# Gate and up units in a seven-product feed-forward: two of four weight sums made by one accumulating transfer, and two small moves beside it

## The chip, the cores and the metric

The kernel runs on one core of a Trainium2 chip. Its time is the device time of one execution in microseconds; lower is better. The engines are called here PE (TensorE), ACT (ScalarE), DVE (VectorE), POOL (GpSimd) and SP (SyncE, which only issues transfers).

## The reference

Two layers of a hybrid decoder trunk on x of 512 rows by 1024 features, in float32. Each layer is

```
x = x + 1/2 * SwiGLU_1(RMSNorm(x))
h = RMSNorm(x);  [conv_a | conv_g | q | k | v] = h @ W_in
x = x + concat(conv_out, diff_out) @ W_out
x = x + 1/2 * SwiGLU_2(RMSNorm(x))

def swiglu(h, w_gate, w_up, w_down):
    return (jax.nn.silu(h @ w_gate) * (h @ w_up)) @ w_down
```

The hidden width of the feed-forwards is 2816, that is 22 tiles of 128. conv_out is a causal depthwise convolution of width 31 behind a gate, diff_out a differential attention with a shared relative-position bias. All matrix products are carried to nearly float32 precision.

## The kernel before

**Products in three parts.** PE multiplies numbers of a rounded 32-bit type (fp32r). So each operand is split into a rounded part (hi, a copy on ACT) and the remainder (lo, a subtraction on DVE), and each product is made as hi by hi, lo by hi and hi by lo. The helper `mm3` (L138, L141, L142) does it for whole tiles of 512 columns, `Unit.product` (L377) for halves of 256 columns.

**A feed-forward** (`ffn`, four in the kernel) has three parts. The first five hidden tiles are plain: a product with the gate and one with the up weights, silu and product on DVE and ACT, hi and lo of the result (`hh`, `hl`: `Gated.plain`, L600 and L601), and eight down products of five tiles each into `ps_d`, added to x at L706. Beside that, `Halves` makes the sums of the two halves of the normed input (L309 to L318), and `settle` its hi and lo parts `acth` and `actl` (L323, L324). Then come two groups, of 8 and of 9 hidden tiles, each followed by four `Down` units. A `GateUp` unit makes one hidden tile's gate and up product with seven products of 256 columns instead of eight, as in Winograd's form of a two by two block product; a `Down` unit does so for two output tiles.

**The weights of a unit.** `GateUp.load` (L455) brings the up weights u and the gate weights g by two transfers of SP, 512 KB each (L457, L458), and POOL makes four sums of them (`sums`, L354 to L357): D = g1 + u1, u1 + u2, u1 + u2 + g1, and that plus g2, where 1 and 2 are the halves of the contracted dimension. `hi` (L363, ACT) and `lo` (L367, DVE) then split the four sets: A (u1 + u2 and u2), B (g), C (the last two sums) and D. Buffers come from rings: `wraw` has five of 128x1024, `whi` and `wlo` four, `wraw2`, `whi2` and `wlo2` (512 wide) two.

**Order.** `Unit.body` (L390) runs one unit and, in between its products, the preparation of the next: load, then hi and lo of A (after the first products, copied at L395), B, D and C. In between go the last product of the unit before (`rest`) and its elementwise work (`finish`, `extras`). Copies of partial sums out of PSUM go to `keep` (L395, L406, L426). A scheduler reorders the instructions of the program by its own model of time; only the first matmul of each product group is held in the order of the program. Each engine runs its stream in order.

**Other places that the steps touch.** `Gated.add` (L607) makes, for the first of a pair of hidden tiles, the difference of the two halves of the activation (L618); the held copy of the activation comes from PSUM one step earlier. `Down.plain` (L540) adds the products of hidden tiles that are in no pair; `middle` (L556) issues the ones for the first bank before the unit's last two product groups. `close` (L565) adds the partial sums (L570) and adds the result to x (L561). The bias table of the attention (`make_bias`) is built beside the first feed-forward; one of its steps is a transfer `d<-d` (L747) on POOL's queue.

Of the kernel before, what the change touches and what calls it, by code (L numbers as in the profile page):

```python
# [14 lines left out]
AF = mybir.ActivationFunctionType  # L15
ALU = mybir.AluOpType
AX = mybir.AxisListType

P = 128
# [27 lines left out]
PIN = False  # L47
# [21 lines left out]
def trunk(ctx: ExitStack, tc: tile.TileContext, xt, par, lamv, relb, onehot,  # L69
          gu1, dn1, wag, wqkv, wout, gu2, dn2, out):  # L70
    nc = tc.nc
    V, S, G, T = nc.vector, nc.scalar, nc.gpsimd, nc.tensor
# [9 lines left out]
    def f32(ap):  # L82
        return ap.bitcast(F32)
# [9 lines left out]
    def ring(tag, n=1024):  # L93
        dt = F32 if "raw" in tag else F32R
        return wp.tile([P, n], dt, tag=tag, name=tag, bufs=RING[tag])
# [70 lines left out]
    for k0, k1 in ((0, 1), (1, 4), (4, KT)):  # L166
        h = slice(k0 * P, k1 * P)
# [48 lines left out]
    class Prep:  # L216


        def __init__(self, l, gain):
            self.l, self.gain = l, gain  # L220
            self.hi, self.lo = acth, actl
            self.s = tmp.tile([P, SEQ], F32, tag="ssum", name="ssum", bufs=1)
# [110 lines left out]
    def pinned(ins, pin=PIN):  # L333
        if pin:
            tc.keep_in_program_order(ins)
        return ins
# [4 lines left out]
    def by_two(t):  # L341
        return t.rearrange("p (n c) -> p n c", n=2)

    class Unit:
# [14 lines left out]
        def hi(self, k, pin=PIN):  # L359
            tag, n = self.WIDE[k]  # L360
            hi, lo = ring("whi" + tag, n), ring("wlo" + tag, n)
            self.parts[k] = hi, lo
            pinned(S.activation(hi[:, : self.cols[k]], self.raw[k][:, : self.cols[k]], AF.Copy), pin)  # L363

        def lo(self, k, pin=PIN):
            (hi, lo), c = self.parts[k], self.cols[k]
            pinned(V.tensor_tensor(out=lo[:, :c], in0=self.raw[k][:, :c], in1=f32(hi[:, :c]), op=ALU.subtract), pin)  # L367
# [22 lines left out]
        def body(self, nxt, prev, prev2):  # L390
            if nxt:
                nxt.load()
            self.begin()
            self.go(self.c, "u2u1", "t1", first=True)
            pinned(S.activation(self.keep[:, 3], self.c, AF.Copy))  # L395
            if nxt:
                nxt.hi("A")
                nxt.lo("A")
            self.go(self.d, "u2", "t4", first=True)
            self.early()  # L400
            if nxt and self.early_free:
                nxt.hi("B")
            if prev:
                prev.rest()
            self.go(self.a, "g1", "b11")
            pinned(S.activation(self.keep[:, :2], by_two(self.banks[0]), AF.Copy))  # L406
            if prev:
                prev.finish(0)
            if nxt and self.early_free:
                nxt.lo("B")  # L410
            if prev:
                prev.finish(1)
            if nxt:
                nxt.hi("D")
                nxt.lo("D")
            if prev:
                prev.finish(2)
            self.go(self.b, "g2", "b21")
            self.middle()
            if nxt:  # L420
                nxt.hi("C")
            if prev2:
                prev2.extras()
            self.go(self.c, "all", "b22")
            self.go(self.a, "g1u2u1", "t2")
            pinned(S.activation(self.keep[:, 2], self.a, AF.Copy))  # L426
            self.close()
            if nxt:
                nxt.lo("C")
                if not self.early_free:  # L430
                    nxt.hi("B")
                    nxt.lo("B")

        early_free = True

        def early(self):
            pass

        def middle(self):
            pass  # L440
# [6 lines left out]

    class GateUp(Unit):
        steps = KT // 2

        def __init__(self, fp, turn, halves, g, u, n, gated):
            super().__init__(fp, turn)
            self.halves, self.src, self.n, self.gated = halves, (g, u), n, gated

        def load(self):  # L455
            u, g = ring("wraw"), ring("wraw")
            nc.sync.dma_start(u, self.src[1])  # L457
            nc.sync.dma_start(g, self.src[0])  # L458
            d, more = ring("wraw2", 512), ring("wraw")
            h = slice(0, 512), slice(512, 1024)  # L460
            self.sums(u[:, h[0]], u[:, h[1]], g[:, h[0]], g[:, h[1]], d, more[:, h[0]], more[:, h[1]])
            self.raw = {"A": u, "B": g, "C": more, "D": d}
            self.cols = {k: n for k, (_, n) in self.WIDE.items()}

        AT = {"u2u1": ("A", 0), "u2": ("A", 4), "g1": ("B", 0), "g2": ("B", 4), "g1u2u1": ("C", 0), "all": ("C", 4),
              "g1u1": ("D", 0)}
# [8 lines left out]
        def close(self):  # L475
            g, two = self.keep[:, 0::2], by_two(self.banks[1])
            pinned(V.tensor_tensor(two, two, g, op=ALU.add))
            pinned(S.activation(g, two, AF.Silu))
# [14 lines left out]
    class Down(Unit):  # L493
# [60 lines left out]
                self.spare()  # L554

        def middle(self):  # L556
            if self.early_free:
                self.plain(self.banks[1], 0)

        def into(self, m, ps, scale):  # L560
# [4 lines left out]
        def close(self):  # L565
            A, B = 2 * self.q, 2 * self.q + 1
            two, keep = by_two(self.banks[1]), self.keep
            if not self.early_free:
                self.plain(self.banks[1], 0)
            pinned(V.tensor_tensor(two, two, keep[:, 0::2], op=ALU.add))  # L570
            self.into(A, two, 0.5)
            self.after(A)
            if not self.early_free:
                self.spare()
            two = by_two(self.ps)
            pinned(V.tensor_tensor(two, two, keep[:, 1::2], op=ALU.subtract))
            self.into(B, two, 0.5)
# [7 lines left out]
    class Gated:  # L585
# [21 lines left out]
        def add(self, n, us, step):  # L607
            a, b = slice(0, HS), slice(HS, SEQ)
            first = self.paired(n) and n % 2 == 0
            if step == 0:  # L610
                if first:
                    self.held[n] = self.fp.tile([P, SEQ], F32, tag=("hh8", "hl8")[n // 2 % 2], name="hold")
                    pinned(S.activation(self.held[n], us, AF.Copy))
                else:
                    self.part_hi(n, us)
            if step == 1:
                if first:
                    pinned(V.tensor_tensor(us[:, b], self.held[n][:, a], self.held[n][:, b], op=ALU.subtract))  # L618
                    self.part_hi(n, us)
                else:  # L620
                    self.part_lo(us)
            if step == 2 and first:
                self.part_lo(us)
# [481 lines left out]
    for l in range(DEPTH):  # L1105
        nxt = {}
# [89 lines left out]
```

## Time and profile before

| | |
|---|---|
| median of the runs | 1791.06 us (1789.68, 1791.06, 1792.72) |
| the profiled execution | 1787.99 us |
| its span | 1786.2 us, 1.8 us less than its time |
| granted clock of PE | 0.999 |
| PE busy | 1771.4 us, 99% |
| DVE, ACT, POOL busy | 1416.0, 960.1 and 950.4 us (79, 54 and 53%) |
| read from HBM | 173.79 MB |

Busy time counts the execution of an engine's instructions. A group's row gives busy time, count and mean, and then the time that the engine sat idle just before, with what ended it. A row of the timeline gives start, duration, engine and line. A row of the waits gives the total, the number of times and the longest, all in us.

### The profile page before, as it was taken

Reading aid. Unit: us, or ns where it says so; the run is one execution under the profiler, and the core shown is the slowest. Engines: PE = TensorE matmul, PEld = TensorE weight load, DVE = VectorE, ACT = ScalarE, POOL = GpSimd, SP = SyncE. Lnnn points to the kernel's source line nnn. Section 1 sums busy time; section 2 is a strip of 40 time slices with the busy share of each in tenths; the row PEclk is TensorE's granted clock in tenths of the full one; section 3 lists DMA queues with packets and bytes.
Section 4 is the critical chain, followed back from the end, with each engine's and each line's share of the span. In section 5 each row is a group of like instructions: output and inputs, shape, how many; then the busy total and the mean of one; then the engine's idle time right before and its main releaser. Section 6 shows DMA issues by size and latency. Waiting matters only on the chain.

```text
span 1786.2 us, 29641 instructions
## 1 busy us (share of the span) xinstructions
PE 1771.4 (99%) x11437; PEld 1608.5 (90%) x11437; DVE 1416.0 (79%) x1949; ACT 960.1 (54%) x1555; POOL 950.4 (53%) x665
## 2 busy tenths in 40 slices
PE   9999999999999999999999999999999999999998
PEld 7899999888788899999888999998877888999997
DVE  6988797768857978798668978976788588887974
ACT  5455465545844456465534654655558354554652
POOL 2275475279952166475304745742798432654750
PEclk9999999999999999999999999999999999999999
DMA  7333334423122233333332333344230232333332
GB/s 224 95 113 97 105 107 113 128 91 95 48 71 83 83 95 118 85 113 120 107 97 71 107 107 99 103 119 130 71 116 26 72 106 73 106 97 105 107 108 70
DMA packets 74222, 177.83 MB, mean 100 GB/s; under 512 B 8951, under 2 KB 30726, under 8 KB 74080
## 3 DMA queue, kind: packets, MB, share of 16 engines
q1 hardware_dynamic: 72480, 174.10, 31.9%
q8 instruction: 89, 1.46, 0.3%
q0 software_dynamic: 1312, 1.67, 0.3%
q14 instruction: 53, 0.43, 0.1%
q10 hardware_dynamic: 288, 0.16, 0.0%
HBM read 173.79 MB, written 3.42 MB: 99 GB/s over the span
## 4 chain that ended last, share of the span: by engine, by line
PE 96%; DVE 2%; ACT 1%; issue 0%; DMA 0%; SPq 0%; DVEq 0%; ACTq 0%
PE ps_pair L377 53%; PE ps_d L377 6%; PE ps_pair L141 5%; PE ps_pair L142 5%; PE ps_pair L138 5%; PE ps_d L138 2%; PE ps_d L142 2%; PE ps_d L141 2%; PE ps_sc L966 2%; PE ps_pair L842 2%; PE ps_pair L843 2%; PE ps_pair L844 2%; PE ps_out L138 1%; PE ps_out L142 1%; PE ps_out L141 1%; PE ps_v L872 1%
## 5 line engine op out<-in xcount | busy, mean ns | idle before, releaser
L367 DVE TENSOR_TENSOR wlo<-wraw,whi 128x1024 fp32r<-128x1024 f32 (+2 forms) x400 | 534.6, 1342 | 122.0 <-ACT whi L363 120.2
L363 ACT ACTIVATE whi<-wraw 128x1024 fp32r<-128x1024 f32 (+2 forms) x400 | 361.5, 909 | 354.6 <-PE ps_pair L377 188.3
L354 POOL TENSOR_TENSOR wraw<-wraw 128x512 f32<-128x512 f32 (+1 forms) x100 | 145.1, 1451 | 540.9 <-DMA wraw<-in_gu 279.4
L377 PE MATMUL ps_pair<-acth,wlo 128*128 128x256 f32 x1088 | 307.9, 283 | 0.0
L377 PE MATMUL ps_pair<-actl,whi 128*128 128x256 f32 x1088 | 307.9, 283 | 0.0
L377 PE MATMUL ps_pair<-acth,whi 128*128 128x256 f32 x1088 | 307.9, 283 | 0.0
L377 PE MATMUL ps_pair<-th,whi 128*128 128x256 f32 x816 | 231.7, 284 | 0.0
L377 PE MATMUL ps_pair<-th,wlo 128*128 128x256 f32 x816 | 230.9, 283 | 0.0
L377 PE MATMUL ps_pair<-tl,whi 128*128 128x256 f32 x816 | 230.9, 283 | 0.0
L377 PEld LDWEIGHTS ps_pair<-acth,whi 128*128 128x128 f32 x1088 | 208.9, 192 | 0.2
L377 PEld LDWEIGHTS ps_pair<-actl,whi 128*128 128x128 f32 x1088 | 208.9, 192 | 0.2
L377 PEld LDWEIGHTS ps_pair<-acth,wlo 128*128 128x128 f32 x1088 | 208.9, 192 | 0.0
L101 ACT ACTIVATE whi<-wraw 128x1024 fp32r<-128x1024 f32 (+3 forms) x124 | 122.6, 999 | 144.4 <-PE ps_pair L141 87.3
L141 PE MATMUL ps_pair<-actl,whi 128*128 128x512 f32 x448 | 174.7, 391 | 0.7 <-DVE actl L227 0.5
L142 PE MATMUL ps_pair<-acth,wlo 128*128 128x512 f32 x448 | 174.1, 390 | 0.0
L138 PE MATMUL ps_pair<-acth,whi 128*128 128x512 f32 x448 | 173.2, 392 | 0.4 <-ACT whi L101 0.4
L356 POOL TENSOR_TENSOR wraw<-wraw 128x512 f32<-128x512 f32 (+1 forms) x100 | 154.0, 1540 | 7.8
L377 PEld LDWEIGHTS ps_pair<-th,whi 128*128 128x128 f32 x816 | 156.6, 192 | 0.9
L357 POOL TENSOR_TENSOR wraw<-wraw 128x512 f32<-128x512 f32 (+1 forms) x100 | 153.2, 1532 | 7.8
L377 PEld LDWEIGHTS ps_pair<-tl,whi 128*128 128x128 f32 x816 | 156.6, 192 | 0.0
L377 PEld LDWEIGHTS ps_pair<-th,wlo 128*128 128x128 f32 x816 | 156.6, 192 | 0.0
L355 POOL TENSOR_TENSOR wraw<-wraw 128x512 f32<-128x512 f32 (+1 forms) x100 | 148.1, 1481 | 7.8
(203 smaller groups left out, 4307.5 us busy)
## 6 DMA issues: line engine op xcount, KB each, us to landing
wraw<-in_gu SPq DMA_DIRECT2D x172, 512.0 KB, 3.6
wraw<-in_wqkv SPq DMA_DIRECT2D x24, 512.0 KB, 3.6
wraw<-in_wag SPq DMA_DIRECT2D x16, 512.0 KB, 3.6
wraw<-in_wout SPq DMA_DIRECT2D x16, 512.0 KB, 3.6
wraw<-in_dn SPq DMA_DIRECT2D x60, 128.0 KB, 3.0
wraw<-in_dn SPq DMA_DIRECT2D x20, 384.0 KB, 3.3
wraw<-in_dn SPq DMA_DIRECT2D x28, 256.0 KB, 2.9
wraw<-in_dn SPq DMA_DIRECT2D x20, 320.0 KB, 3.1
```

Source lines behind the costliest of these rows:

```text
L101: S.activation(hi, raw, AF.Copy)
L138: first = T.matmul(ps, wh, xh, start=start, stop=False)
L141: T.matmul(ps, wh, xl, start=False, stop=False)
L142: T.matmul(ps, wl, xh, start=False, stop=stop)
L354: G.tensor_tensor(d, g1, u1, op=ALU.add)
L355: G.tensor_tensor(u1, u1, u2, op=ALU.add)
L356: G.tensor_tensor(m0, u1, g1, op=ALU.add)
L357: G.tensor_tensor(m1, m0, g2, op=ALU.add)
L363: pinned(S.activation(hi[:, : self.cols[k]], self.raw[k][:, : self.cols[k]], AF.Copy), pin)
L367: pinned(V.tensor_tensor(out=lo[:, :c], in0=self.raw[k][:, :c], in1=f32(hi[:, :c]), op=ALU.subtract), pin)
L377: mm = T.matmul(ps, l, r, start=first and i == n == 0, stop=False, skip_group_check=True)
L842: T.matmul(ps[n], xh[:, t], wh, start=k == 0, stop=False)
```

## The change

`GateUp.load` issues four transfers of SP: gate's first half and up's second half into the two halves of a buffer `two`, the whole gate weights into `g`, and up's second half once more into a 512-wide buffer. One transfer on POOL's queue then adds up's first half to both halves of `two` while it is written, which gives D and the first half of A. POOL makes the two remaining sums. A now lies in two buffers, and its hi and lo are made in two instructions of 512 columns each. For units that prepare a `GateUp` unit, the hi and lo of A come later in the body, behind `finish(1)` and ahead of D. The difference at L618 (L646 after) takes its second operand from PSUM instead of from the held copy. In the last `Down` unit of each feed-forward the plain products of the first bank are issued in `close` and not in `middle`.

```diff
--- before.py
+++ after.py
@@ -393,7 +393,7 @@
             self.begin()
             self.go(self.c, "u2u1", "t1", first=True)
             pinned(S.activation(self.keep[:, 3], self.c, AF.Copy))
-            if nxt:
+            if nxt and nxt.soon:
                 nxt.hi("A")
                 nxt.lo("A")
             self.go(self.d, "u2", "t4", first=True)
@@ -411,6 +411,9 @@
             if prev:
                 prev.finish(1)
             if nxt:
+                if not nxt.soon:
+                    nxt.hi("A")
+                    nxt.lo("A")
                 nxt.hi("D")
                 nxt.lo("D")
             if prev:
@@ -432,6 +435,7 @@
                     nxt.lo("B")
 
         early_free = True
+        soon = True
 
         def early(self):
             pass
@@ -447,20 +451,44 @@
 
     class GateUp(Unit):
         steps = KT // 2
+        soon = False
 
         def __init__(self, fp, turn, halves, g, u, n, gated):
             super().__init__(fp, turn)
             self.halves, self.src, self.n, self.gated = halves, (g, u), n, gated
 
         def load(self):
-            u, g = ring("wraw"), ring("wraw")
-            nc.sync.dma_start(u, self.src[1])
-            nc.sync.dma_start(g, self.src[0])
-            d, more = ring("wraw2", 512), ring("wraw")
             h = slice(0, 512), slice(512, 1024)
-            self.sums(u[:, h[0]], u[:, h[1]], g[:, h[0]], g[:, h[1]], d, more[:, h[0]], more[:, h[1]])
-            self.raw = {"A": u, "B": g, "C": more, "D": d}
-            self.cols = {k: n for k, (_, n) in self.WIDE.items()}
+            gate, up = self.src
+            two, g, u2 = ring("wraw"), ring("wraw"), ring("wraw2", 512)
+            nc.sync.dma_start(two[:, h[0]], gate[:, h[0]])
+            nc.sync.dma_start(two[:, h[1]], up[:, h[1]])
+            nc.sync.dma_start(g, gate)
+            nc.sync.dma_start(u2, up[:, h[1]])
+            nc.gpsimd.dma_start(
+                by_two(two), up[:, h[0]].unsqueeze(1).broadcast_to([P, 2, 512]), accum_op=ALU.add
+            )
+            more = ring("wraw")
+            G.tensor_tensor(more[:, h[0]], two[:, h[1]], g[:, h[0]], op=ALU.add)
+            G.tensor_tensor(more[:, h[1]], more[:, h[0]], g[:, h[1]], op=ALU.add)
+            self.raw = {"A": (two[:, h[1]], u2), "B": (g,), "C": (more,), "D": (two[:, h[0]],)}
+
+        def pieces(self, k):
+            at = 0
+            for raw in self.raw[k]:
+                n = raw.shape[1]
+                yield raw, *(p[:, at : at + n] for p in self.parts[k])
+                at += n
+
+        def hi(self, k, pin=PIN):
+            tag, n = self.WIDE[k]
+            self.parts[k] = ring("whi" + tag, n), ring("wlo" + tag, n)
+            for raw, hi, _ in self.pieces(k):
+                pinned(S.activation(hi, raw, AF.Copy), pin)
+
+        def lo(self, k, pin=PIN):
+            for raw, hi, lo in self.pieces(k):
+                pinned(V.tensor_tensor(out=lo, in0=raw, in1=f32(hi), op=ALU.subtract), pin)
 
         AT = {"u2u1": ("A", 0), "u2": ("A", 4), "g1": ("B", 0), "g2": ("B", 4), "g1u2u1": ("C", 0), "all": ("C", 4),
               "g1u1": ("D", 0)}
@@ -554,7 +582,7 @@
                 self.spare()
 
         def middle(self):
-            if self.early_free:
+            if self.early_free and not self.last:
                 self.plain(self.banks[1], 0)
 
         def into(self, m, ps, scale):
@@ -565,7 +593,7 @@
         def close(self):
             A, B = 2 * self.q, 2 * self.q + 1
             two, keep = by_two(self.banks[1]), self.keep
-            if not self.early_free:
+            if not self.early_free or self.last:
                 self.plain(self.banks[1], 0)
             pinned(V.tensor_tensor(two, two, keep[:, 0::2], op=ALU.add))
             self.into(A, two, 0.5)
@@ -615,7 +643,7 @@
                     self.part_hi(n, us)
             if step == 1:
                 if first:
-                    pinned(V.tensor_tensor(us[:, b], self.held[n][:, a], self.held[n][:, b], op=ALU.subtract))
+                    pinned(V.tensor_tensor(us[:, b], self.held[n][:, a], us[:, b], op=ALU.subtract))
                     self.part_hi(n, us)
                 else:
                     self.part_lo(us)
```

## Prediction

> **What bounds the kernel now.** I read the page's busy times and chain first, then the list of what TensorE (PE) waits for, then the longest pieces of the chain, then the grouped rows of the engines that the change touches, and last the timeline at the places where the order changes.
>
> ```profile
> PE 1771.4 (99%) x11437; PEld 1608.5 (90%) x11437; DVE 1416.0 (79%) x1949; ACT 960.1 (54%) x1555; POOL 950.4 (53%) x665
> PE 96%; DVE 2%; ACT 1%; issue 0%; DMA 0%; SPq 0%; DVEq 0%; ACTq 0%
> PE ps_pair L377 <- ACT keep L426: 3.2, 3, 1.4
> PE ps_v L872 <- ACT qz L888: 1.8, 1, 1.8
> 90.65 87.87 PE ps_pair L377 x720
> ```
>
> PE is busy 99% of the span and is 96% of the chain. The fifth line is a stretch of the gate/up units: 720 half-width products in 87.87 us, 0.122 us each without a gap, so a unit of 7 x 12 = 84 products takes 10.25 us, whatever VectorE (DVE), ScalarE (ACT), GpSimd (POOL) and the transfers do underneath. The change removes and adds no product. It can gain only what PE waits for, of which the largest entry is the 3.2 us before L377, and it can lose without limit if a weight or an activation comes late.
>
> **The moved plain products: the gain.** The last Down unit of each feed-forward sends its plain products (5 x 3 at 128x512) ahead of the last pair's reconstruction; after the change they stand between the copy L426 (L429 after) and the last products that need it.
>
> ```profile
> 316.99 3.43 PE ps_d L377 x15
> 350.90 0.28 PE L377 MATMUL ps_pair<-hs,wlo 128*128 128x256 f32 x1
> 352.54 0.50 PE L377 MATMUL ps_pair<-hs,whi 128*128 128x256 f32 x2 [1.35 <-ACT keep L426]
> 1780.90 0.50 PE L377 MATMUL ps_pair<-hs,whi 128*128 128x256 f32 x2 [0.47 <-ACT keep L426]
> 1780.88 0.70 DVE L570 TENSOR_TENSOR ps_pair<-ps_pair,keep 128x512 f32<-128x512 f32 x1 [3.94 <-ACT keep L426]
> 356.70 2.69 POOL L239 TENSOR_TENSOR ssum<-ssum,sq 128x512 f32<-128x512 f32 x2 [2.21 <-ACT sq L235]
> 360.19 0.60 PE L196 MATMUL ps_rows<-ident,ssum 128*128 128x128 f32 x4
> ```
>
> The first line sizes the moved block, 3.43 us of PE. At 350.90 PE waits 1.35 us for the copy, and the same 1.35 us comes again in layer 1 (3.2 = 1.35 + 1.35 + 0.47). A block of 3.43 us covers it, so both waits go: -2.7 us. What is late next there is the row of squares: PE's transposes of it ran at 360.19 and POOL's last sum (L239) ends at 359.39; that chain also moves up, so I count the gain as whole and its loss (0 of 2.7) as the lower bound. At the end of the kernel the final subtraction L570 starts when the copy is there (1780.88); after the change it is PE that ends last, at about 1780.45 without its wait of 0.47, so 0.4 us at most and 0.3 taken. At the fourth place, the passage from layer 0 to layer 1, no wait stands in the list, so nothing. Sum -3.0 us, at least 0, at most -3.4.
>
> **PSUM instead of SBUF for one difference (L618).**
>
> ```profile
> L618 DVE TENSOR_TENSOR ps_pair<-hold 128x256 f32<-128x256 f32 x16 | 24.4, 1522 | 0.0
> L484 DVE TENSOR_TENSOR ps_pair<-ps_pair,keep 128x256 f32<-128x256 f32 x68 | 28.6, 421 | 0.1
> ```
>
> The same shape with a PSUM operand takes 421 instead of 1522 ns: 16 x 1.1 = 17.6 us of DVE. DVE is not on the chain there, since PE runs these stretches without a gap: nothing.
>
> **The four sums and the accumulating transfer.**
>
> ```profile
> L354 POOL TENSOR_TENSOR wraw<-wraw 128x512 f32<-128x512 f32 x68 | 116.8, 1717 | 370.6 <-DMA wraw<-in_gu 279.4 <-issue 35.7 <-DVE wlo L367 21.6
> L357 POOL TENSOR_TENSOR wraw<-wraw 128x512 f32<-128x512 f32 x68 | 125.5, 1845 | 5.3
> L367 DVE TENSOR_TENSOR wlo<-wraw,whi 128x1024 fp32r<-128x1024 f32 x268 | 396.1, 1480 | 103.3 <-ACT whi L363 101.9
> L367 DVE TENSOR_TENSOR wlo<-wraw,whi 128x512 fp32r<-128x512 f32 x116 | 125.6, 1083 | 18.7 <-ACT whi L363 18.3
> L363 ACT ACTIVATE whi<-wraw 128x1024 fp32r<-128x1024 f32 x268 | 283.9, 1060 | 281.4 <-PE ps_pair L377 138.6 <-PE ps_d L377 56.8 <-POOL wraw L356 26.5
> L363 ACT ACTIVATE whi<-wraw 128x512 fp32r<-128x512 f32 x116 | 72.9, 628 | 67.5 <-PE ps_pair L377 44.1 <-POOL wraw L354 16.9 <-DVE wlo L367 2.7
> q1 hardware_dynamic: 72480, 174.10, 31.9%
> wraw<-in_gu SPq DMA_DIRECT2D x172, 512.0 KB, 3.6
> d<-brow POOLq DMA_DIRECT2D x1, 8.0 KB, 1.7
> d<-d POOLq DMA_DIRECT2D x1, 1280.0 KB, 19.7
> ```
>
> In each of 68 units POOL loses two of four sums and keeps about 3.6 us (two of these rows). A's hi and lo in two halves cost ACT 2 x 0.63 for 1.06 (+0.2 us a unit) and DVE 2 x 1.08 for 1.48 (+0.7, less what two fewer POOL sums give back). Both have room: nothing. SP issues four loads of 1.25 MB for two of 1 MB, and with the accumulating 0.5 MB a unit moves 1.75 times as much; the hardware queue takes 31.9% of the 16 engines now, so bandwidth is there. What is new is that POOL issues a transfer and waits for it before its two sums, and that it issues the next only after them. With L the time from issue to landing, POOL's loop lasts L + 3.6 and must not exceed 10.25: L up to 6.65 costs no lag at all. No accumulating transfer is in the trace. From below: a plain hardware transfer of the size takes 3.6. From above: the one large transfer on POOL's queue took 19.7 us for 1280 KB, 7.9 for 512 KB, and with 1.7 for a small one 9.6. I take 5.5: 1.7 fixed, and two reads of 512 KB at the 1.9 us (3.6 less 1.7) of one. This lies under 6.65, so in the steady stretch nothing, and the range keeps the upper end.
>
> The row that this leans on is the 3.6 us of a plain transfer. The Trainium skill, page "Collectives: The Full Stack", section "The bandwidth ceiling: the fold count and why AG ≠ RS ≠ AR", says that an adding transfer reads two sources through one ring and so moves at half the rate (62.28 against 32.35 GB/s there). By it alone the data part would double, the L that I take; no run here shows it yet.
>
> There is also lead before a lag hurts. The row order of one unit:
>
> ```profile
> 114.88 1.45 DVE L367 TENSOR_TENSOR wlo<-wraw,whi 128x512 fp32r<-128x512 f32 x1
> 113.12 0.58 ACT L478 ACTIVATE keep<-ps_pair 128x512 f32<-128x512 f32 x1
> ```
>
> A unit's first pair is now loaded when this lo of D frees its buffer (116.3), lands 3.6 later (119.9), and A's hi is due right after the L478 slot (113.7) two bodies on, at 134.2: 14.3 us, some 16.5 with the 2.3 us that I estimate ACT can slip. A transfer of L plus lags of L - 6.65 over 5 (group of eight) or 6 (group of nine) loops must fit: L up to 8.3 and 8.1.
>
> **The start of a feed-forward: the cost.** The instruction streams say where the first unit's D is converted. In the first feed-forward its hi on ACT, and its lo on DVE, now stand ahead of the plain weights' hi (L101), of the plain units' hh (L600) and of the hi of the normed activations; before they stood behind hh. Both engines run in order, so all of that now waits for the first accumulating transfer.
>
> ```profile
> 44.76 1.15 POOL L747 DMA_DIRECT2D d<-d  x1 [1.75 <-DMA d<-brow]
> 64.78 1.85 POOL L354 TENSOR_TENSOR wraw<-wraw 128x512 f32<-128x512 f32 x1 [18.87 <-DMA wraw<-in_gu]
> 50.33 0.33 SPq L457 DMA_DIRECT2D wraw<-in_gu  x1
> DMA to landing us min/median/max: 3.4/3.6/12.4
> 58.79 0.61 ACT L600 ACTIVATE hh<-gs 128x512 fp32r<-128x512 f32 x1
> 66.67 0.63 ACT L363 ACTIVATE whi<-wraw 128x512 fp32r<-128x512 f32 x1 [3.71 <-POOL wraw L354]
> 64.65 0.62 PE L138 MATMUL ps_d<-hh,whi 128*128 128x512 f32 x2
> 65.78 0.39 PE L141 MATMUL ps_d<-hl,whi 128*128 128x512 f32 x1
> L102 DVE TENSOR_TENSOR wlo<-wraw,whi 128x1024 fp32r<-128x1024 f32 x67 | 86.1, 1292 | 37.1 <-ACT whi L101 37.1
> L633 DVE TENSOR_TENSOR hl<-ps_pair,hh 128x512 fp32r<-128x512 f32 x68 | 46.3, 680 | 5.3 <-ACT hh L628 5.3
> ```
>
> The unit's load at 50.33 is the slow one (12.4 us, landed 62.7), beside the bias table's d<-d, which is on POOL's queue from 44.76 to 64.46. The accumulating transfer can only be asked for at 62.7 or a little later and stands behind d<-d on the same queue. It lands at X: at the earliest 64.5 + 1.7 = 66.2, at the latest 64.5 + 5.5 = 70; I take 68.5. From X follow D's hi (0.6), its lo (1.1), the weights' lo (L102, 1.3) and hl (L601, 0.7 as L633): hl is there at X + 3.7, and PE, which read it at 65.78, stands X - 62.1 = 6.4 us (4.1 to 7.9). The hi side, X + 2.2 against 64.65, gives 6.0. These are waits of PE that nothing hides: +6.4 us.
> ```profile
> 1501.52 0.63 ACT L600 ACTIVATE hh<-gs 128x512 fp32r<-128x512 f32 x1 [7.12 <-DVE gs L689]
> 1502.73 1.07 PE L138 MATMUL ps_d<-hh,whi 128*128 128x512 f32 x4
> ```
>
> At the other three starts no bias table is in the way and the load lands in 3.6 us. The tightest tile there is the last hh, ready at 1502.15 and read among the four products from 1502.73, so with about 0.8 us of slack: 0 to 1 us each, I take +0.5 in all.
>
> The two mixers' products come in another order in the stream as well (a scheduler places them); the largest of PE's waits there is the 1.8 us of the row quoted first, so I put this at 0, from -1.5 to +2.
>
> **Sum.** -3.0 + 6.4 + 0.5 = +3.9 us on the profiled execution (span 1786.2, 1.8 around it, 1787.99). It lies 3.1 under the median of the runs, 1791.06; I add the difference to the median: **1795.0 us**. About 0.2% (3.6 us) is what a measurement of this kernel can tell from no change.
>
> **Rivals.**
> 1. No stall at the start (0.2): the transfer gets ahead of the tail of d<-d, or lands by 62.5 or so because the pair's loads are smaller. Then the gain is alone: 1791.06 - 3.0 = 1788.0, with a friendly mixer order 1786.5. Against it: the 12.4 us and d<-d's end at 64.46.
> 2. The accumulating transfer is slow (0.17): L beyond 8.1 makes POOL's loop the bound in all four feed-forwards. At L = 8.5 a group of eight is late by 51.0 - 49.8 = 1.2, of nine by 59.5 - 56.4 = 3.1, four of each 17 us: on top of the forecast, 1812. At 9.6 it is 7.8 + 10.8, times four 74 us: 1869. For it: the d<-d row. Against: that transfer's outermost dimension is short, the new one runs over 128 partitions.
> 3. The start stalls but less, X at 66.2 (0.2): 4.1 instead of 6.4, with mixers at -1: 1791.
>
> Forecast as above, 0.43: 1793 to 1798. Faster by over 0.2% needs both no stall and a good order of the mixers, or the gain at the passages larger than its waits: 0.18. Within 0.2%: 0.27 (most of rival 3 and the rest of rival 1, the low part of the forecast). Slower: 0.55 (the rest of the forecast, rival 2). The range, 1787.0 to 1812, leaves out the good end of rival 1 and most of rival 2.
>
> **What would show it.** Right: in the list of PE's waits the entry for the copy L429 shrinks to under 0.6 us, and a new one of 4 to 8 us stands before ps_d L138 or L141 near 65 us, put down to hh or hl; the gate/up stretch stays at 87.87 us; the DMA issues show the accumulating transfer at 5 to 6 us. Wrong: no gap near 65 (rival 1), or PE gaps before L377 that recur from unit to unit, released by whi L487, with the landing above 8 us (rival 2). A shift in the mixers at equal waits would mean that the order of their products counted for more than I gave it.

## The result, and the profile after

The changed kernel takes 1808.95 us, median of five runs (1808.36 to 1811.45), against 1790.19 us (1789.17 to 1792.72) for the kernel before: a ratio of 1.0109, 95% interval 1.0097 to 1.0120. It is 18.8 us slower; 1795.0 was forecast, with a range from 1787.0 to 1812.

The page of the changed kernel, busy times and chain:

```profile
PE 1778.5 (98%) x11437; PEld 1610.4 (89%) x11437; DVE 1329.0 (74%) x2017; ACT 963.6 (53%) x1623; POOL 768.6 (43%) x597
PE 87%; DVE 6%; DMA 5%; issue 1%; ACT 1%; SPq 0%; DVEq 0%; POOLq 0%; ACTq 0%
```

POOL lost 182 us of work and DVE 87 us, and the kernel became slower: neither was what it waited for. The chain now spends 11% on DVE and transfers, where before PE had nearly all of it. That is not 11% lost, since PE worked beside most of it. What PE waits for (total, times, longest), changed kernel:

```profile
PE ps_d L138 <- ACT hh L628: 8.7, 3, 7.1
PE ps_d L138 <- DVE x L734: 4.8, 3, 2.7
PE ps_v L900 <- ACT qz L916: 1.8, 1, 1.8
```

The 3.2 us on the copy L429 are gone. Two new entries stand before `ps_d`, the plain down products at the start of a feed-forward. The long pieces of the chain show that nothing happened inside the groups:

```profile
51.50 12.64 DMA wraw<-in_gu
64.83 5.69 DMA wraw<-in_gu
88.88 5.63 DMA wraw<-in_gu
105.26 87.87 PE ps_pair L377 x720
```

720 products still take 87.87 us; they begin at 105.26 instead of 90.65. The three lines ahead of it are what stands in the way: the first unit's load, its accumulating transfer, and the second unit's accumulating transfer.

Both kernels run the same number of products on PE, outside the mixers almost in the same order. So the start times can be subtracted product by product. By how much each stretch is longer than in the kernel before (minus: shorter), in us, profiled executions of the changed kernel and of the experiments:

```
                     changed  small_  accum_  sums_   sums_   move_   bias_   late_d
                              edits   only    first1  first2  some    wide
before 49.5 us          0.80    1.80    1.79    0.06    0.08    0.45    0.04    0.87
start, 1st ff          13.82    0.00   12.27    2.29    0.00    0.00    7.81    0.00
its end                -1.62   -1.61    0.00   -1.62   -1.62   -1.61   -1.61   -1.61
mixer, layer 0          0.40    1.05    0.67    1.01    2.82    1.90    2.49    1.47
start, 2nd ff           2.02    0.00    1.73    0.21    0.00    0.00    2.34    0.00
start, 3rd ff           1.57    0.00    2.31    0.81    0.00    0.00    1.87    0.00
its end                -1.61   -1.61    0.00   -1.61   -1.61    0.00   -1.61   -1.61
mixer, layer 1          2.19    3.85   -0.05    2.17    2.19   -0.09    2.20    3.87
start, 4th ff           3.28    0.00    2.27    0.06    0.00    0.00    2.57    0.00
end                    -0.73   -0.73    0.00   -0.73   -0.73   -0.73   -0.73   -0.73
```

The groups of units and the stretch between the layers have no row, since they differ by 0.03 or less each. For the changed kernel the column sums to 20.1 us: 20.7 at the four starts, -4.0 at the three ends, 2.6 in the mixers and 0.8 in the first 50 us, where executions differ by up to 2 us among themselves. It is the ledger that the experiments below are read from.

The first start in the timelines of the changed kernel: POOL, then ACT, DVE and PE.

```profile
64.83 1.29 POOL L468 DMA_DIRECT2D wraw<-in_gu  x1 [18.19 <-DMA wraw<-in_gu]
88.88 1.21 POOL L468 DMA_DIRECT2D wraw<-in_gu  x1 [12.06 <-DVE actl L324]
```

```profile
70.55 0.63 ACT L487 ACTIVATE whi<-wraw 128x512 fp32r<-128x512 f32 x1 [15.05 <-DMA wraw<-in_gu]
71.08 1.04 ACT L101 ACTIVATE whi<-wraw 128x1024 fp32r<-128x1024 f32 x1
72.03 0.61 ACT L628 ACTIVATE hh<-gs 128x512 fp32r<-128x512 f32 x1
94.54 0.63 ACT L487 ACTIVATE whi<-wraw 128x512 fp32r<-128x512 f32 x1 [4.72 <-DMA wraw<-in_gu]
```

```profile
95.20 0.69 DVE L491 TENSOR_TENSOR wlo<-wraw,whi 128x512 fp32r<-128x512 f32 x1 [3.92 <-ACT whi L487]
95.81 1.88 DVE L734 SCALAR_TENSOR_TENSOR x<-ps_d,x 128x512 f32<-128x512 f32 x3
```

```profile
72.69 1.22 PE L138 MATMUL ps_d<-hh,whi 128*128 128x512 f32 x2 [7.09 <-ACT hh L628]
96.54 0.50 PE L138 MATMUL ps_d<-hh,whi 128*128 128x512 f32 x1 [2.68 <-DVE x L734]
```

ACT stands still for 15 us until the transfer issued at 64.83 has landed, then does D's hi, the weights' hi and hh, which was ready to be made before 60. That is the wait that was forecast. The second one was not: at 94.54 ACT, and with it DVE, wait in the same way for the second unit's transfer, and behind DVE's lo (L491) stand the additions of `ps_d` to x (L734) that free PE's banks.

### The profile page after: what moved, and what is told of

Its sections match the earlier page's. It is cut to its first block, busy times and chain, and to the rows that moved or that the text cites. A ratio compares the mean times of both kernels' runs of the same rounds, so it can differ in the third digit from the quotient of the medians.

```text
span 1807.0 us, 30275 instructions
## 1 busy us (share of the span) xinstructions
PE 1778.5 (98%) x11437; PEld 1610.4 (89%) x11437; DVE 1329.0 (74%) x2017; ACT 963.6 (53%) x1623; POOL 768.6 (43%) x597
## 4 chain that ended last, share of the span: by engine, by line
PE 87%; DVE 6%; DMA 5%; issue 1%; ACT 1%; SPq 0%; DVEq 0%; POOLq 0%; ACTq 0%
PE ps_pair L377 52%; PE ps_d L377 5%; DMA wraw<-in_gu 5%; PE ps_pair L141 4%; PE ps_pair L142 4%; PE ps_pair L138 4%; PE ps_sc L994 2%; PE ps_pair L870 2%; PE ps_pair L872 2%; PE ps_pair L871 2%; PE ps_out L138 1%; PE ps_out L142 1%; PE ps_out L141 1%; DVE wlo L102 1%; DVE actl L324 1%
## 5 line engine op out<-in xcount | busy, mean ns | idle before, releaser
L491 DVE TENSOR_TENSOR wlo<-wraw,whi 128x512 fp32r<-128x512 f32 (+1 forms) x340 | 341.2, 1019 | 177.1 <-ACT whi L487 176.1
L487 ACT ACTIVATE whi<-wraw 128x512 fp32r<-128x512 f32 (+1 forms) x340 | 263.8, 798 | 267.9 <-PE ps_pair L377 178.1
L472 POOL TENSOR_TENSOR wraw<-wraw 128x512 f32<-128x512 f32 x68 | 93.4, 1373 | 382.3 <-DMA wraw<-in_gu 276.1
L363 ACT ACTIVATE whi<-wraw 128x1024 fp32r<-128x1024 f32 (+2 forms) x128 | 103.6, 818 | 159.9 <-PE ps_pair L377 80.0
L367 DVE TENSOR_TENSOR wlo<-wraw,whi 128x1024 fp32r<-128x1024 f32 (+2 forms) x128 | 125.0, 984 | 71.3 <-ACT whi L363 70.9
L468 POOL DMA_DIRECT2D wraw<-in_gu x68 | 81.9, 1205 | 194.1 <-DMA wraw<-in_gu 113.6
```

The costliest lines, as they stand in the source:

```text
L468: nc.gpsimd.dma_start(by_two(two), up[:, h[0]].unsqueeze(1).broadcast_to([P, 2, 512]), accum_op=ALU.add)
L472: G.tensor_tensor(more[:, h[0]], two[:, h[1]], g[:, h[0]], op=ALU.add)
L487: pinned(S.activation(hi, raw, AF.Copy), pin)
L491: pinned(V.tensor_tensor(out=lo, in0=raw, in1=f32(hi), op=ALU.subtract), pin)
```

## The experiments

**The two small edits alone.**

```diff
 kernel before
-            if self.early_free:                    # middle
+            if self.early_free and not self.last:
-            if not self.early_free:                # close
+            if not self.early_free or self.last:
-  ... us[:, b], self.held[n][:, a], self.held[n][:, b], op=ALU.subtract ...
+  ... us[:, b], self.held[n][:, a], us[:, b], op=ALU.subtract ...
```

> The kernel before with only the two small edits: the plain products of the last Down unit moved and the difference reading PSUM; the four sums stay on POOL. Theory 1 (all of the loss comes from the accumulating transfers at the starts of the feed-forwards): 1787 us, 3 us less than before, from the two waits of 1.35 us on the copy and a little at the end. Rival 2 (the moved products reorder the second mixer, where the changed kernel lost 2 us more): 1789 us, the gain of 3 less those 2.

1789.04 us against 1789.68, ratio 0.9994 (0.9985 to 1.0003): no difference that can be told. The ledger says why: -1.6, -1.6 and -0.7 at the ends, somewhat more than forecast, and +3.85 in layer 1's mixer, +1.05 in layer 0's.

**The accumulating transfers without the moved products.**

```diff
 changed kernel
-            if self.early_free and not self.last:
+            if self.early_free:
-            if not self.early_free or self.last:
+            if not self.early_free:
```

> The changed kernel with the plain products put back into middle; accumulating transfers and the PSUM difference stay. Theory 1: the two waits of 1.35 us on the copy are back, about 1812 us, 3 more than the changed kernel. Rival 2 (the second mixer's order comes from the moved products): the 2 us there go as the 3 come back, about 1810.

1808.81 us, ratio 1.0104 (1.0090 to 1.0118): the same as the changed kernel, nearer to rival 2's 1810 than to 1812. The 4 us at the ends are lost, layer 1's mixer is back at -0.05, and the first start costs 1.6 us less. So the moved products gave nothing in the whole, and the loss comes with the accumulating transfers. The 1.6 us at the first start are not the move's: PE's waits there sum to 9.4 us instead of 9.8, and the granted clock, 0.50 behind both waits in the changed kernel (97.1 to 100.4 the second time), falls here only behind the first.

**Who of the 68 units causes it.** First one, then two units of each feed-forward make their four sums on POOL again.

```diff
 changed kernel
+            for unit in units[:2]:      # units[:1] in the other
+                unit.old = unit.soon = True
             units[0].load()
 ...
         def load(self):
+            if self.old:
+                return self.load_sums()  # load and sums of the kernel before
```

> The changed kernel, but the first gate/up unit of each feed-forward (4 of 68) makes its four sums on POOL as before; all others use the accumulating transfer. Theory 1: the stall of 7.2 us and the slow products behind it in the first feed-forward go (some 9 us), while the later stall there (2.8 us) and the ones of about 1 us at the other starts, which I put to the second unit's transfer, stay: about 1799 us. Rival 3 (the cost is spread over all transfers, by traffic or contention, and only shows at the starts): nearly no change, 1807 or more.

> The changed kernel, but the first two gate/up units of each feed-forward (8 of 68) make their four sums on POOL as before. Theory 1: all stalls at the starts go, what stays is the gain of the small edits, perhaps less 2 us in the second mixer: 1787 to 1790 us. Rival 3 (cost spread over all transfers): 1800 or more, since 60 of 68 transfers remain.

With one: 1793.18 us, ratio 1.0017 (1.0008 to 1.0026), 6 us better than expected. With two: 1789.47, ratio 0.9996 (0.9987 to 1.0004). Taken out in this order, the first units' 4 transfers carry some 15.8 us, the second units' 3.7, the other 60 nothing. Rival 3 (cost spread over all) falls. My split was off: I had put the later stall, up to 96.54, to the second unit, but it is largely the first one's doing: the whole start costs 2.29 us when the first unit comes in time.

**Only the place of the conversions.** All 68 accumulating transfers stay; D of the first unit is converted in program order behind the plain hh and hl.

```diff
 changed kernel, Gated.plain and ffn
-            S.activation(hi, us, AF.Copy)
-            V.tensor_tensor(lo, us, f32(hi), op=ALU.subtract)
+            pinned(S.activation(hi, us, AF.Copy), True)
+            pinned(V.tensor_tensor(lo, us, f32(hi), op=ALU.subtract), True)
-            for k in "ABDC":
-                units[0].hi(k, False)
-                units[0].lo(k, False)
+            for k in "DABC":
+                units[0].hi(k, k == "D")
+                units[0].lo(k, k == "D")
```

> The changed kernel with all 68 accumulating transfers; only the hi and lo of the first unit's D are held in program order behind the plain units' hh and hl, so that on ACT and DVE they stand behind them and behind the last weights of the plain down products. Theory 1 (the loss is the place of these conversions in the in-order streams, not the transfers): the stalls before ps_d go; the second unit's D still stands ahead of the first unit's A on ACT, which may leave 0 to 2 us at each start: 1789 to 1797 us. Rival 3 (the transfers themselves cost it, by traffic or latency): over 1804.

1790.21 us, ratio 1.0001 (0.9992 to 1.0010): all four starts are at 0.00 in the ledger. ACT and the waits of PE in this kernel:

```profile
59.66 0.61 ACT L628 ACTIVATE hh<-gs 128x512 fp32r<-128x512 f32 x1
60.70 0.61 ACT L628 ACTIVATE hh<-gs 128x512 fp32r<-128x512 f32 x1
80.06 0.61 ACT L487 ACTIVATE whi<-wraw 128x512 fp32r<-128x512 f32 x1
84.99 3.57 ACT L487 ACTIVATE whi<-wraw 128x512 fp32r<-128x512 f32 x5 [4.32 <-DMA wraw<-in_gu]
```

```profile
PE ps_v L900 <- ACT qz L916: 1.8, 1, 1.8
PE ps_sc L994 <- DVE e L1008: 1.4, 3, 0.7
```

hh is made at 59.66 and 60.70 again, D's hi only at 80.06. ACT still waits 4.3 us for the second unit's transfer, but nothing that PE needs soon stands behind it. No entry for `ps_d` is left. The same transfers, the same bytes, another place in two in-order streams: that is the whole loss.

**Why the first transfer is so late.** The bias table's d<-d is written with 128 rows outermost.

```diff
 changed kernel, make_bias
-  nc.gpsimd.dma_start(d2, d1.unsqueeze(1).broadcast_to([HEADS, P, RLEN]))
+  nc.gpsimd.dma_start(d2.rearrange("h p r -> p h r"), d1.unsqueeze(0).broadcast_to([P, HEADS, RLEN]))
```

> The changed kernel with the bias table's d<-d written with 128 rows outermost instead of 512 merged from 4 heads, nothing else. Theory A (this transfer holds few of the 16 engines for 18 us, so the first unit's load takes 12.6 us and the accumulating transfer is asked for late): d<-d is done in under 8 us, the load at 51.5 lands by 57, the accumulating transfer by 64, and the stall of 7.2 us with the slow products behind it goes: about 1800 us. Rival B (the load is slow for the sake of its neighbours on the hardware queue): the load still takes over 10 us and the time stays at 1808.

1802.97 us, ratio 1.0077 (1.0063 to 1.0091). The DMA issues, POOL's timeline and PE's timeline:

```profile
d<-d POOLq DMA_DIRECT2D x1, 1280.0 KB, 8.3
```

```profile
57.16 1.27 POOL L468 DMA_DIRECT2D wraw<-in_gu  x1 [11.75 <-DVE gs L717]
```

```profile
66.20 0.73 PE L138 MATMUL ps_d<-hh,whi 128*128 128x512 f32 x2 [1.35 <-ACT hh L628]
89.79 0.50 PE L138 MATMUL ps_d<-hh,whi 128*128 128x512 f32 x1 [2.48 <-DVE x L734]
```

d<-d takes 8.3 us (18.4 in the changed kernel), the accumulating transfer goes out 7.7 us earlier, and the first wait shrinks from 7.1 to 1.35 us. The load itself lands after 5.7 us (50.74 to 56.47) instead of 12.6. So the bias table did make the load late (theory A). Behind the first wait PE waits 1.5 us more for hl, and the second wait stays, since the order stays; 6 of the 14 us at this start are gone, 3 fewer than I expected.

**Idle products in the pause.**

```diff
 changed kernel, the plain down products
+                    if lead and m == 0 and kk == 2:
+                        idle(bank("y", "ps_fill"), 30)
                     mm3(ps, wpart(w, b % 8), h.hh[kk], ...)   # held in program order up to there
```

> The changed kernel with 30 idle products of 128x512 (6.9 us) on PE just ahead of the product that waits 7.2 us in the first feed-forward; they need nothing and write a bank that nobody reads. Theory C (after the pause PE runs at about half its clock for some 4 us, and that is a cost of the pause itself): the granted clock from 72.5 to 77 is 1.0 instead of 0.55, products there come every 0.23 us instead of 0.43, and the kernel is 1.9 us faster than the changed one. Rival D (the slow products wait for data): they stay at 0.43 us, no gain.

1813.17 us, ratio 1.0141 (1.0125 to 1.0157): 4 us worse, neither theory's number. The windows of the changed kernel around its pause, and of this one (us, PE busy, PEld, DVE, ACT, POOL, granted PE clock, DMA share, GB/s):

```profile
65.00:72.60 7.60, 0.60 (x3) 0.18 (x1) 1.14 (x2) 2.06 (x4) 1.12 (x1) 0.81 0.43 69
72.60:74.60 2.00, 1.91 (x5) 1.52 (x6) 2.00 (x3) 2.00 (x5) 1.13 (x1) 0.50 0.00 0
74.60:76.60 2.00, 2.00 (x6) 1.61 (x5) 2.00 (x2) 2.00 (x4) 1.92 (x2) 0.51 0.00 0
76.60:78.60 2.00, 2.00 (x10) 1.58 (x10) 2.00 (x4) 2.00 (x4) 0.22 (x1) 1.00 0.00 0
```

```profile
72.00:74.00 2.00, 1.12 (x4) 0.67 (x4) 2.00 (x3) 2.00 (x4) 1.18 (x1) 1.00 0.00 0
74.00:76.00 2.00, 0.34 (x2) 0.00 (x0) 2.00 (x2) 2.00 (x5) 1.92 (x2) 0.65 0.00 0
76.00:78.00 2.00, 1.26 (x3) 1.06 (x4) 2.00 (x4) 2.00 (x5) 0.14 (x1) 0.50 0.00 0
```

In the changed kernel the clock is 0.50 for 4 us behind the pause. With the pause filled it is 1.00 behind it, as theory C has it, but then PE waits for hl for 2.4 us and drops to 0.50 after that. The kernels differ in more than the filling, since holding the products in program order also fixed that the third tile's hl is used before later hi products. So what the slow clock costs by itself stays open; the operands were late anyway.

**How much delay the steady stretch bears.** A second accumulating transfer in every unit from the third on: in the first kernel one that POOL's two sums don't read, in the second one that they do.

```diff
 the kernel with two units on sums
             nc.gpsimd.dma_start(by_two(two), up[:, h[0]]..., accum_op=ALU.add)
+            nc.gpsimd.dma_start(two[:, h[0]], up[:, h[0]], accum_op=ALU.add)   # slow_accum
+            nc.gpsimd.dma_start(two[:, h[1]], up[:, h[0]], accum_op=ALU.add)   # slow_sums
```

> As the kernel whose first two units make their sums on POOL, but every other gate/up unit adds up's first half once more to the first half of its buffer, by a second accumulating transfer that waits for the first. D then is g1 + 2 u1, so the result is another one. Theory E (a loop of POOL is L + 3.6 us and may last 10.25, and the lead of a group bears L up to about 8): L becomes 5.9 + 4.3 = about 10.2, a loop 13.8; by the prediction's formula a group of eight is late by 11.5 and a group of nine by 15, times four 106 us: about 1895 us, with PE gaps before L377 that recur with each unit. Rival F (the transfers are hidden whatever they take): 1790 us.

> As the kernel whose first two units make their sums on POOL; every other gate/up unit adds up's first half a second time to the second half of its buffer, which the two sums read, so that POOL has to wait for both transfers. A and C hold another sum then, and the result is another one. The earlier slowed kernel had a loop of only 10.6 us, since its second transfer was not waited for. Theory E (loop of L + 3.6 against 10.25): L about 5.9 + 5.0 = 11, loop 14.6; by the prediction's formula 16 and 21 us late per group of eight and nine, times four about 150 us: 1940 us. Rival F (the lead of a group is larger than the formula has it): PE gaps recur before L377, but the sum stays under 75 us.

1802.01 and 2004.67 us, one run each. My expectation for the first was wrong in its dose: POOL doesn't wait for a landing that its sums don't read. Waits of PE in the first and in the second, then POOL's timeline in the second:

```profile
PE ps_pair L377 <- ACT keep L406: 7.6, 12, 1.9
```

```profile
PE ps_pair L377 <- ACT keep L406: 137.9, 52, 5.1
PE ps_pair L377 <- ACT keep L429: 5.5, 17, 0.5
```

```profile
108.88 1.20 POOL L480 DMA_DIRECT2D wraw<-in_gu  x1
122.76 1.21 POOL L480 DMA_DIRECT2D wraw<-in_gu  x1
136.62 1.20 POOL L480 DMA_DIRECT2D wraw<-in_gu  x1
151.05 1.21 POOL L480 DMA_DIRECT2D wraw<-in_gu  x1
165.67 1.21 POOL L480 DMA_DIRECT2D wraw<-in_gu  x1
```

The loop of the second lasts 14.2 us on average (165.67 less 108.88, over four), and each feed-forward's groups lose 50.9, 51.8, 62.3 and 52.5 us, 218 in all. PE's waits are 143 us of that. The rest is clock: the granted clock of this execution is 0.963 against 0.999 before, which is 72 us of 2003. So with a long enough loop POOL does become the bound. In the first, where a loop lasted 10.4 to 10.9, the groups lost 2.5 to 4.3. That it is the loop there too is not shown, since ACT also stood still for the second transfer ahead of D's hi (2.6 us at 116.84, 4.0 at 160.45), where in the changed kernel D's hi found its data ready. The changed kernel, at L = 5.9 and some 9.8 us a loop where POOL waits only for its transfer, is below 10.25. Rival F falls in the second. The first, at 1802, lies nearer to rival F's 1790 than to theory E's 1895, whose dose it did not get.

**The moved products at fewer places.** The small edits alone, without the move in layer 1's first feed-forward.

```diff
 kernel with the two small edits
-  end and q == KT // 2 - 1))
+  end and q == KT // 2 - 1 and move))    # move: False for gu1 of layer 1
```

> The two small edits alone, but the plain products are not moved in the first feed-forward of layer 1, whose successor is the second mixer. There PE's order is then that of the kernel before. Theory (the move itself gains 1.5 us at each end, and in the second mixer the other order that the scheduler chooses costs more): the second mixer takes the time of before, the waits on the copy stay at that one place, sum -1.6 in layer 0, +0.4 to +1 in the first mixer, -0.7 at the end: 1788 us. Rival (the second mixer's loss in these profiles is chance): no better than with the move at all places, 1789.

1788.73 us, ratio 0.9999 (0.9991 to 1.0008). Layer 1's mixer, now in the order of before, is at -0.09 where every kernel with the move stood at +2.2 or +3.9. Product by product PE's order there is that of before, as in the kernel with the accumulating transfers alone (-0.05); with the move 365 of 1257 positions hold another product, and PE's waits there sum to 4.1 us instead of 2.9. So the move causes the mixer's loss, by the scheduler's other order. No difference to the kernel before can be told here either, and no version tried beats it.

## Why the prediction was right and where it was short

**The number.** All four signs of a right forecast came: no wait on the copy, a wait of 7.1 us before `ps_d` for hh, 87.87 us for the 720 products, and 5.9 us for the transfer. But +3.9 us was forecast and +18.8 came. That 1808.95 lies within the range is luck: the upper end, 1812, was kept for rival 2, a transfer too slow for the groups, and that did not happen.

**What bounds the kernel: right.** PE's pace in the groups did not change by a hundredth, and 269 us less work on DVE and POOL bought nothing.

**The moved products: right in place, given back elsewhere.** 1.6 us were gained at each of the two passages (1.35 forecast). At the end PE's last product comes 0.73 us earlier, but the final subtraction, on which the end hangs, only 0.34 (1801.40, less the 20.86 of the rows above, against 1780.88; 0.3 forecast). That makes -3.6, where -3.0 was forecast. The step that failed is "I put this at 0, from -1.5 to +2" for the mixers: layer 1's mixer costs 2.2 us in its other order, in six profiles alike; in the two at 3.9 the granted clock was 0.94 over some 29 us from 1320 on, 1.00 in the kernel before and in the changed one. Layer 0's 0.4 to 2.8 go mostly with the clock. In the changed kernel it is 1.00 there, and 0.4 us are lost. In the kernel with the move at fewer places it is 0.50 from 498.9 to 502.3 (1.9 us lost), and with two units on sums from 496.8 to 503.6 (2.8 lost). The accumulating transfers alone, in exactly the order of before, lose 0.7 with 0.50 from 512.2 to 515.5. Why one execution has such a stretch and another has not stays open.

**The PSUM operand: right.** Changed kernel, the grouped rows:

```profile
L646 DVE TENSOR_TENSOR ps_pair<-hold,ps_pair 128x256 f32<-128x256 f32 x16 | 6.7, 418 | 0.0
L491 DVE TENSOR_TENSOR wlo<-wraw,whi 128x512 fp32r<-128x512 f32 x204 | 140.9, 716 | 65.1 <-ACT whi L487 64.8
L473 POOL TENSOR_TENSOR wraw<-wraw 128x512 f32<-128x512 f32 x68 | 124.8, 1835 | 5.3
wraw<-in_gu POOLq DMA_DIRECT2D x68, 512.0 KB, 5.9
```

418 ns, 421 forecast. The halves of lo took 716 ns, not the 1083 of the row that I took. The traces tell why. Lo has both operands in SBUF; before, 76 of the 116 ran half of their time or more beside a sum of POOL and took 1290 ns on average, and the 39 beside none took 688. After the change 179 of 204 run beside none and take 681. The difference at L618 is the same case: with both operands in SBUF and 81% of its time beside a sum it took 1522 ns, and with one in PSUM, in the kernel with the small edits alone and wholly beside a sum, 416.

**The accumulating transfer's length: right.** 5.9 us, 5.5 forecast, so no lag in the groups. The two-reads rule of the Trainium skill ("Collectives: The Full Stack", section "The bandwidth ceiling: the fold count and why AG ≠ RS ≠ AR") fits: 2.3 us more than the plain 3.6, where a second read of the data part was put at 1.9. No run here separates the reads from a longer fixed part. The formula for a late group held roughly where it was tried: a loop of 14.2 (L of 10.6) costs 14 + 18 = 32 us for each feed-forward by it, and PE waited 36. What it leaves out is the clock that fell between the waits; with it the loss was 54.

**The first start: right in kind, half in size.** The transfer landed at 70.5 (64.83 + 5.69; 68.5 taken, 70 the latest), and the wait was 7.1 us (6.4). The step that failed is that the account ended there. Behind the wait stood products at half the clock, and a second wait of 2.7 us for the second unit's transfer, again with products at half the clock behind it: 9.8 us of waits and 4.0 of slower products, so that this start cost 13.8 us.

**The other starts: the wrong term.** "0 to 1 us each, I take +0.5 in all" measured 2.0, 1.6 and 3.3, together 6.9. I looked at hh and its slack alone. hh's waits were in fact 0.9 us at the second and 0.8 at the fourth start; the additions L734 behind DVE's conversions added 0.7 at the third and 1.4 at the fourth, and the lo of the weights (L102) 0.2 at each of the three. That is 4.4 us; the other 2.5 come in the first two products behind each wait, some 0.3 us for each, at a granted clock of 1.00. With that the sum would have been -3.6 + 13.8 + 6.9 + 2.6 = 19.7, near the 18.8 measured. Rival 1 (no stall), rival 2 (the transfer too slow for the groups) and rival 3 (a stall of 4.1 us) all fall by the ledger and the waits.

## What to carry to other kernels

A change that makes an instruction wait for something new has its price in what stands behind that instruction on its engine, not in how long the new thing takes: with 68 slower preparations the kernel lost 19 us, all of it through the eight at stage starts, and nothing once the first of each start was put behind work that PE needed. Follow the wait through every in-order engine it touches, and for the second unit as well as the first. And an edit that moves one block under a scheduler can reorder a stage 100 us later; subtract the start times of all products before crediting the edit.

## What was not expected of the hardware

After a pause of 7.1 us the granted clock of PE was 0.50 for 4 us and then 1.00 at once; among waits of 0.2 to 0.8 us in the mixer of layer 0 it fell to 0.50 for 3.4 or 6.8 us in some executions and not in others. The transfer d<-d of 1280 KB took 18.4 us with 4 heads and 128 rows merged outermost and 8.3 us with 128 rows outermost. A subtraction on DVE with both operands in SBUF took 688 ns alone and 1290 beside POOL's sums; one of half the size with an operand in PSUM took 414 to 424 ns beside a sum and 417 and 422 beside none.
